# Row 0 of the first tile loaded from GpSimd's queue beside the other rows on SP's queue

## Chip, cores, metric

The kernel runs on one core of a Trainium2 chip. Times are device microseconds (us) of one launch; medians are given. The span of a profile is about 1.9 us shorter than the time of the same run. Kernels are compared only within the same rounds.

## The reference, cut to what matters

```python
# x: 1024 x 4096 float32, axis = -1
mean = np.mean(x, axis=axis, keepdims=True)
return ((x - mean) ** 2).astype(np.float32)
```

16.78 MB are read and 16.78 MB written, for very little arithmetic.

## The kernel before

There are two tiles of 128 partitions; each partition holds four rows (q = 0 to 3) of 4096 numbers, 64 KB. Both tiles are loaded at once, one DMA each ("load 1", "load 2"). VectorE sums a row, a tiny VectorE instruction turns the sum into the negative mean, ScalarE squares the row in place with the mean as bias. After rows 1 and 3 of each tile half a tile is stored: stores 1 and 2 of tile 1, 3 and 4 of tile 2. SP issues all of them into one queue. The loops, shortened:

```python
for i in range(ntiles):                      # ntiles = 2
    x_tile = io.tile([P, Q * D], F32)        # P = 128, Q = 4, D = 4096
    nc.sync.dma_start(out=x_tile, in_=x_t[i])
    tiles.append(x_tile)

for i in range(ntiles):
    for q in range(Q):
        row = tiles[i][:, q * D:(q + 1) * D]
        # ... neg_sum, neg_mean: [P, 1] tiles
        nc.vector.reduce_sum(out=neg_sum, in_=row, axis=..., negate=True)
        nc.vector.tensor_scalar_mul(out=neg_mean, in0=neg_sum, scalar1=inv_d)
        nc.scalar.activation(out=row, in_=row, func=Square, bias=neg_mean, scale=1.0)
        if q % H == H - 1:                   # H = 2
            part = slice((q + 1 - H) * D, (q + 1) * D)
            nc.sync.dma_start(out=out_t[i][:, part], in_=tiles[i][:, part])
```

Of the kernel before, what the change touches and what calls it, by code (L numbers as in the profile page):

```python
# [2 lines left out]

os.environ.setdefault("NEURON_RT_ULTRASERVER_MODE", "4")

# [4 lines left out]

F32 = mybir.dt.float32


@with_exitstack
def kernel(
    ctx: ExitStack,
    tc: tile.TileContext,
    x: bass.AP,
    axis: bass.AP,
    out: bass.AP,  # L20
):


    nc = tc.nc

    B, D = x.shape
    P = nc.NUM_PARTITIONS
    Q = 4
    H = 2
    assert B % (P * Q) == 0  # L30
    ntiles = B // (P * Q)
    inv_d = 1.0 / float(D)

    x_t = x.rearrange("(n p q) d -> n p (q d)", p=P, q=Q)
    out_t = out.rearrange("(n p q) d -> n p (q d)", p=P, q=Q)

    io = ctx.enter_context(tc.tile_pool(name="io", bufs=ntiles))
    stats = ctx.enter_context(tc.tile_pool(name="stats", bufs=2 * ntiles * Q))

    tiles = []  # L40
    for i in range(ntiles):
        x_tile = io.tile([P, Q * D], F32)
        nc.sync.dma_start(out=x_tile, in_=x_t[i])  # L43
        tiles.append(x_tile)

    for i in range(ntiles):
        for q in range(Q):
            row = tiles[i][:, q * D:(q + 1) * D]
            neg_sum = stats.tile([P, 1], F32)
            neg_mean = stats.tile([P, 1], F32)  # L50
            nc.vector.reduce_sum(  # L51
                out=neg_sum, in_=row, axis=mybir.AxisListType.X, negate=True
            )
            nc.vector.tensor_scalar_mul(out=neg_mean, in0=neg_sum, scalar1=inv_d)  # L54
            nc.scalar.activation(  # L55
                out=row,
                in_=row,
                func=mybir.ActivationFunctionType.Square,
                bias=neg_mean,
                scale=1.0,  # L60
            )
            if q % H == H - 1:
                part = slice((q + 1 - H) * D, (q + 1) * D)
                nc.sync.dma_start(out=out_t[i][:, part], in_=tiles[i][:, part])


# [1 line left out]
_INS = ['x', 'axis']  # L68
_OUTS = [((1024, 4096), 'float32')]

_NUMBERS = {'axis': -1}


# [26 lines left out]
```

## Time and profile before

| | before |
|---|---|
| time, median | 83.22 us |
| VectorE busy, of the span | 35.4 us, 44% |
| ScalarE busy | 30.7 us, 38% |
| DMA engines busy (mean of 16) | 96.2% |
| load 1 in, VectorE starts | 22.50 us |
| store 1 issued | 39.46 us |

Read it from the DMA side. The compute engines have gaps of many microseconds, the DMA engines none between 1.75 and 80.2 us. The prediction shows the lines. In the trace a "packet" is one contiguous piece that one of the 16 DMA engines moves, here one partition's part of a load or store. The records don't name the engine; a packet is put to the engine whose packet before ended as this one began. The engines pass from load 2 to store 1 at about 41.3 us.

### The profile page before, as it was taken

How to read it: one execution, taken by the hardware profiler on the slowest of the kernel's cores; microseconds unless marked ns; L12 is line 12 of the kernel's file. 1: busy time of each engine (PE TensorE's matmuls, PEld its weight loads, DVE VectorE, ACT ScalarE, POOL GpSimd, SP SyncE). 2: the span in 40 equal slices, each digit the busy share in tenths (PEclk: the TensorE clock that was granted, in tenths of full speed). 3: DMA queues.
4: the chain of work that ended last, by engine and by line, in shares of the span. 5: the costliest groups of instructions: out<-in, count | busy, mean ns of one | idle time of the engine just before them, and what ended most of it. 6: DMA issues, size and time to landing. Idle time of an engine off the chain costs nothing.

```text
span 81.3 us, 79 instructions
## 1 busy us (share of the span) xinstructions
DVE 35.4 (44%) x16; ACT 30.7 (38%) x9; POOL 0.2 (0%) x4
## 2 busy tenths in 40 slices
DVE  0000000000099999999749999999920000000000
ACT  0000000000060005969699930979879980000000
POOL 0000000000000000000000000000000000000000
DMA  9399947999965999992997997997998998898990
GB/s 387 129 516 516 516 193 322 516 516 516 516 290 226 516 516 516 516 483 129 419 516 306 467 516 322 451 516 338 435 516 354 419 516 387 387 516 387 403 500 0
DMA packets 864, 33.55 MB, mean 413 GB/s; under 512 B 96, under 2 KB 96, under 8 KB 96
## 3 DMA queue, kind: packets, MB, share of 16 engines
q1 hardware_dynamic: 864, 33.55, 96.2%
HBM read 16.78 MB, written 16.78 MB: 412 GB/s over the span
## 4 chain that ended last, share of the span: by engine, by line
DMA 50%; DVE 22%; ACT 5%; ACTq 4%; SPq 0%; issue 0%
DMA x_tile<-in_x_dram 50%; DVE neg_sum L51 21%; ACT x_tile L55 5%; ACTq L95 4%; SPq L43 0%; DVE neg_mean L54 0%
## 5 line engine op out<-in xcount | busy, mean ns | idle before, releaser
L51 DVE TENSOR_REDUCE neg_sum<-x_tile 128x1 f32<-128x4096 f32 x8 | 35.0, 4413 | 24.1 <-DMA x_tile<-in_x_dram 24.1
L55 ACT ACTIVATE x_tile<-x_tile,neg_mean 128x4096 f32<-128x4096 f32 x8 | 29.4, 3704 | 13.5 <-DVE neg_mean L54 13.5
L55 ACT ACT_TABLE_LOAD x1 | 1.3, 1283 | 22.5 <-DMA x_tile<-in_x_dram 22.5
L54 DVE TENSOR_SCALAR neg_mean<-neg_sum 128x1 f32<-128x1 f32 x8 | 1.1, 148 | 0.0
L81 POOL MEMSET const-bfloat16-1.0<- 128x1 bf16 x1 | 0.1, 101 | 0.0
L81 POOL MEMSET const-uint8-127<- 128x1 uint8 x1 | 0.1, 101 | 0.0
L81 POOL MEMSET const-float32-0.0<- 128x1 f32 x1 | 0.1, 98 | 0.2 <-issue 0.2
L81 POOL MEMSET const-float32-1.0<- 128x1 f32 x1 | 0.1, 98 | 0.0
## 6 DMA issues: line engine op xcount, KB each, us to landing
out_dram<-x_tile SPq DMA_DIRECT2D x4, 4096.0 KB, 12.9
x_tile<-in_x_dram SPq DMA_DIRECT2D x2, 31.2
```

The costliest lines, as they stand in the source:

```text
L51: nc.vector.reduce_sum(out=neg_sum, in_=row, axis=mybir.AxisListType.X, negate=True)
L54: nc.vector.tensor_scalar_mul(out=neg_mean, in0=neg_sum, scalar1=inv_d)
L55: nc.scalar.activation(out=row, in_=row, func=mybir.ActivationFunctionType.Square, bias=neg_mean, scale=1.0,)
L81: nc = _bacc.Bacc("TRN2", target_bir_lowering=False, num_devices=1)
L95: with _tile.TileContext(nc) as tc:
```

## The change

Its intent is that row 0 comes in early, so that VectorE can start before the whole tile is there.

```diff
-        nc.sync.dma_start(out=x_tile, in_=x_t[i])
+        if i == 0:
+            nc.gpsimd.dma_start(out=x_tile[:, :D], in_=x_t[i][:, :D])
+            nc.sync.dma_start(out=x_tile[:, D:], in_=x_t[i][:, D:])
+        else:
+            nc.sync.dma_start(out=x_tile, in_=x_t[i])
```

## The prediction

> **What bounds the kernel now.** I read the page from the top (busy shares, the slices, the DMA queue, the chain), then SP's waits, then the timeline, then the trace's records of single DMA packets. The first question for a load-compute-store kernel is whether its DMA engines ever run dry, because that decides whether an earlier start of the compute can be worth anything.
>
> ```profile
> DVE 35.4 (44%) x16; ACT 30.7 (38%) x9; POOL 0.2 (0%) x4
> ...
> DVE  0000000000099999999749999999920000000000
> ACT  0000000000060005969699930979879980000000
> POOL 0000000000000000000000000000000000000000
> DMA  9399947999965999992997997997998998898990
> ...
> DMA packets 864, 33.55 MB, mean 413 GB/s; under 512 B 96, under 2 KB 96, under 8 KB 96
> ...
> q1 hardware_dynamic: 864, 33.55, 96.2%
> ```
>
> No compute engine is busy for half of the span; the 16 DMA engines are busy for 96.2% of it, which is 0.962 x 81.3 = 78.2 us. Digits of 2, 3 or 4 in the DMA row look like holes. They are not: the packets are long against a slice of 2.03 us, and a slice in which few packets begin reads low while its neighbour reads too high. The packet records settle it. The loads are 256 packets of 64 KB (one per partition and tile), the stores 512 of 32 KB; the other 96 are the 4-byte semaphore writes, one per engine and transfer. A 64 KB packet takes 2.418 us (27.1 GB/s for an engine, 434 for 16), a 32 KB packet 1.213 us. The first packet of an engine begins between 1.75 and 2.27 us, and from there every engine's next packet begins at the end of the one before (a 64 KB packet every 2.414 us, no gap), through both loads and all four stores, until the last data packet ends at 80.2 us. The check: 33.55 MB in 80.2 - 1.75 = 78.45 us is 428 GB/s, 98.6% of 434. So one unbroken DMA stream sets the end.
>
> Next, what the compute engines wait for, and what SP, which issues everything, waits for. The chain of waits:
>
> ```profile
> by line: DMA x_tile<-in_x_dram 50.0%; DVE neg_sum L51 21.4%; ACT x_tile L55 4.6%; ACTq L95 4.4%; SPq L43 0.5%; DVE neg_mean L54 0.2%; issue 0.2%
> ```
>
> The same view piece by piece (start, length, what), which must be read with care:
>
> ```profile
> 1.16 40.64 DMA x_tile<-in_x_dram
> 41.80 0.02 issue
> 41.83 8.75 DVE neg_sum L51 x2
> ...
> 59.45 3.71 ACT x_tile L55
> 63.15 3.60 ACTq L95
> ```
>
> It ends at 66.8 us, at ACT's last Square, and leaves out the 13.4 us of stores after it. Taken literally it says that VectorE's sums cost 21% of the path. SP's waits (total, times, longest) show what is missing, the stores at the end, 13.3 us in the last line:
>
> ```profile
> SPq L64 <- ACT x_tile L55: 43.1, 4, 16.9
> SPq L64 <- DMA x_tile<-in_x_dram: 20.9, 1, 20.9
> SPq L95 <- DMA out_dram<-x_tile: 13.3, 2, 9.6
> ```
>
> Last, the timeline, for the first tile and the stores:
>
> ```profile
> 0.73 0.86 SPq L43 DMA_DIRECT2D x_tile<-in_x_dram  x2
> 22.50 8.75 DVE L51 TENSOR_REDUCE neg_sum<-x_tile 128x1 f32<-128x4096 f32 x2 [22.50 <-DMA x_tile<-in_x_dram]
> ...
> 39.46 27.65 SPq L64 DMA_DIRECT2D out_dram<-x_tile  x4
> ...
> 41.83 8.75 DVE L51 TENSOR_REDUCE neg_sum<-x_tile 128x1 f32<-128x4096 f32 x2 [1.62 <-DMA x_tile<-in_x_dram]
> ```
>
> The first store is issued at 39.46 us, while the engines still drain load 2 (to 41.4), so it is behind no hole. I check the other three by the ends of Square on ACT: store 2 at 40.11 + 7.31 = 47.4, store 3 at 55.06 + 3.71 = 58.8, store 4 at 66.8. The engines finish load 2 at 41.4, store 1 at 51.1, store 2 at 60.8, store 3 at 70.5 (8 packets x 1.213 = 9.7 us each). Each store is issued before its predecessor is through, with 1.9, 3.7, 2.0 and 3.7 us to spare. Compute is hidden, if narrowly.
>
> **What the Trainium skill says.** Four places, all on the page "DMA: Bandwidth & Descriptors". (1) Section "Issuing engines are not separate DMA queues": transfers started by the different engines run on the same 16 DMA engines and interleave; issuing from several saves sequencer time only. The trace has one queue, so it neither confirms nor denies this; what issuing could save is small, 0.86 us for both loads. (2) Section "Queues, rings and completion order": a DMA engine takes turns between the queues that have work, a whole packet at a time. Not shown here yet. (3) Section "Latency and other measured facts": about 0.6 us to the first byte for SP's path, about 1 us for GpSimd's. In the trace SP's issue begins at 0.73 and the first packet at 1.75, 1.0 us; GpSimd's has no example. (4) Section "Where 436 GB/s comes from": a ceiling of 435 GB/s for the 16 engines. The trace agrees: 434.
>
> **The change part by part.** Bytes: none added, none removed. Load 1 (8.39 MB as 128 packets of 64 KB) becomes 128 packets of 48 KB on SP's queue and 128 of 16 KB on GpSimd's; load 2 and the stores stay. At 27.1 GB/s a 48 KB packet is 1.81 us and a 16 KB one 0.605, together the 2.42 of before. Per engine that is 8 packets more, 24 instead of 16 for the loads. On one queue a further packet costs no gap that the trace shows; for the further packets and the turns between two queues I allow 0.01 (a semaphore write takes 0.009) to 0.05 us each, 8 times: 0.1 to 0.4 us. That is my choice, nothing in the trace measures it. 16 semaphore writes more at 9 ns cost nothing. SP still issues two loads, at about 0.4 us each; the third is issued on GpSimd, which has nothing else to do after its four memsets, done at 0.43 us.
> Start: SP's first packets leave at 1.75 as before, so the engines have work from then on whatever GpSimd does: 0. The first packet of an engine took 2.61 to 3.35 us, 3.06 in the mean, 0.64 over 2.418. A second queue could fill some of that start-up, so at best 0.5 us are won.
> Middle: row 0 lands early or not (below), VectorE may take its sum before 22.5, and then rows 1 to 3 end up to 4.4 us sooner. The instruction order also changes: the first mean follows the first sum at once, where before it came after the second. The most that comes of it is that store 1 is issued at about 35.0 (a sum of row 1 from 22.3, of row 2 to 31.1, a mean 0.14, Square 3.71) instead of 39.46. It stands behind load 2 on SP's queue, which drains to 41.4 either way. Worth: 0. Tile 2 starts at 41.8 when load 2 lands, unchanged, and so do stores 3 and 4.
> End: last packet at 80.2, then 1.1 us to the end of the span. A GpSimd queue in use may cost something in set-up or tear-down outside the stream; I allow 0 to 0.3.
> Sum: 83.22 + 0.25 (packets, queue turns) - 0.2 (start-up) + 0.1 = about 83.4.
>
> **The rivals.** First, when does row 0 land? Each engine has 8 small and 8 large packets. If it alternates whole packets, row 0 needs nearly all turns: 2.0 + 0.64 + 8 x 2.42 = 22.0 us, or 1.8 less if the small packet goes first in each turn; with some 0.4 to the wait's end, 20.5 to 22.4, and the intent of the change fails. If the two queues share by bytes, row 0 is through after twice its 8 x 0.605: 2.0 + 0.64 + 9.7 = 12.3. If a turn drains all of GpSimd's descriptors, about 2.0 + 3.06 + 4.8 = 10. I hold the first likeliest, as the profile counts a partition's row as one packet. All three leave the time where it is.
> Second, a gain from compute (4.4 us, to 78.8): the chain of waits speaks for it, VectorE's sums stand in it with 21%; the unbroken packets speak against it. It needs the DMA stream to have holes, and there is at most 1.0 us between the stream's 78.45 us and 33.55 MB at 434 GB/s, 77.4. So even the best stream gives 82.2, less than 2%.
> Third, GpSimd's queue is a burden: descriptors made late or in small pieces, a DMA engine that lags and holds back the last store. Only 2.1 of 33.55 MB are moved by it, 4.8 us of an engine's time; 20% worse would be 1.0 us, 84.2. Even arriving 10 us late costs nothing, since SP's queue fills the engines; it would only delay row 0, for which tile 1 has 1.9 us to spare.
>
> **Range and chances.** 83.4, with 82.8 (start-up filled, turns free) to 84.2 (third rival) for 8 in 10. Faster by over 2% needs below 81.6, which is less than the fastest stream allows: 0.01. Slower by over 2% needs 84.9, a small-packet cost of 1.7 us: 0.03. Within 2%: 0.96.
>
> **What would show it.** Right: DMA share of busy near 96%, some 94 to 97; two queues, GpSimd's with 2.1 MB; the last Square still near 66.8; VectorE waiting for load 2 until about 41.8; the first store issued between 35 and 40. Row 0's landing tells which rule of turns holds. Wrong: gaps between packets after row 0; stores that begin after their predecessor has drained; first packets much later than 1.75; an end longer than 1.1 us after the last packet.

## The result

The changed kernel takes 85.22 us (85.04 to 85.28), the kernel before in the same rounds 83.19. The ratio is 1.0237 (95% interval 1.0212 to 1.0261): slower. Ratios here are the mean time of one kernel's fast runs over that of the other's of the same rounds, so not quite the ratio of the medians quoted.

The page of the changed kernel, slices and queues:

```profile
DVE  0000000000008999999999999999900000000000
...
DMA  9299999977999659999059599979959996995990
...
DMA packets 1008, 33.55 MB, mean 402 GB/s; under 512 B 112, under 2 KB 112, under 8 KB 112
...
q1 hardware_dynamic: 864, 31.46, 88.2%
q0 software_dynamic: 144, 2.10, 5.9%
```

The bytes are the same. VectorE starts one slice later than before, not sooner. The two queues together are busy for 94.1% of a longer span, 78.6 us, against 78.2 before: the engines do the same work and have idled about 2 us more. A digit in the DMA row that is low only because few long packets begin in a slice looks the same as a real hole, so the row alone doesn't show where. The timeline of the changed kernel (start, length, engine, line, operation, and what ended the idle time):

```profile
1.22 0.65 POOL L44 DMA_DIRECT2D x_tile<-in_x_dram  x1 [0.78 <-PEq L99]
25.27 4.42 DVE L55 TENSOR_REDUCE neg_sum<-x_tile 128x1 f32<-128x4096 f32 x1 [25.27 <-DMA x_tile<-in_x_dram]
...
38.62 3.71 ACT L59 ACTIVATE x_tile<-x_tile,neg_mean 128x4096 f32<-128x4096 f32 x1 [5.00 <-DVE neg_mean L58]
42.36 25.93 SPq L68 DMA_DIRECT2D out_dram<-x_tile  x4
```

Row 0's sum starts at 25.27 instead of 22.50, 2.77 us later, and store 1 is issued at 42.36 instead of 39.46, 2.90 later. (The rest, 0.12, is the first mean, which now sits between the first two sums.) The issues with their times to landing say which load was late:

```profile
x_tile<-in_x_dram SPq DMA_DIRECT2D x1, 6144.0 KB, 21.5
x_tile<-in_x_dram POOLq DMA_DIRECT2D x1, 2048.0 KB, 24.0
x_tile<-in_x_dram SPq DMA_DIRECT2D x1, 41.0
```

The 2 MB of row 0 took longer to land than the 6 MB of rows 1 to 3. And this is the stretch around the passage from loads to stores, first in the kernel before, then in the changed one (window, length, busy time of VectorE, ScalarE and GpSimd with counts, clock, DMA share, GB/s):

```profile
41.30:43.20 1.90, 1.37 (x1) 1.90 (x1) 0.00 (x0) 1.00 0.96 414
43.20:80.20 37.00, 16.34 (x8) 18.94 (x6) 0.00 (x0) 1.00 0.98 425
```

```profile
41.30:43.20 1.90, 1.90 (x4) 1.22 (x2) 0.00 (x0) 1.00 0.00 0
43.20:82.30 39.10, 17.51 (x8) 21.84 (x6) 0.00 (x0) 1.00 1.00 429
```

For 1.9 us no data packet begins in the changed kernel. The packet records, as the mean of the 16 engines: loads done at 41.31 (before 41.26), first store packet at 43.26 (before 41.28), hence a hole (time of an engine between its last load packet and its first store packet) of 1.95 us against 0.01; the stores then take 38.95 us (before 38.74); the last one is done at 82.21 (before 80.01). So of 2.20 us in the profiled runs, 1.95 are the hole, 0.21 slightly slower stores, 0.05 the loads.

The chain of waits of the changed kernel gives VectorE's sums 41.6%, of the kernel before 21.4%:

```profile
by line: DVE neg_sum L55 41.6%; DMA x_tile<-in_x_dram 28.8%; ACT x_tile L59 4.4%; ACTq L99 4.3%; issue 0.8%; DVE neg_mean L58 0.7%; POOLq L99 0.0%; POOLq L85 0.0%
```

VectorE's busy time is 35.4 us in both. The chain follows VectorE further back because it no longer waits for load 2; it doesn't say that the sums cost more.

Why row 0 was late can be followed on one DMA engine. These are its packets in the changed kernel, put together from the trace's packet records (queue 1 is SP's, 0 GpSimd's; 4 B is the semaphore write that says "this engine's share has landed"):

```
1.761 to 4.115    queue 1  49152 B
4.111 to 5.929    queue 1  49152 B
5.925 to 6.536    queue 0  16384 B      first of row 0
6.532 to 8.347    queue 1  49152 B
...                                     strictly in turn
18.626 to 20.441  queue 1  49152 B      eighth and last of rows 1 to 3
20.438 to 21.049  queue 0  16384 B      seventh of row 0
21.045 to 21.054  queue 1  4 B          rows 1 to 3 done
21.051 to 21.662  queue 0  16384 B      eighth of row 0
21.658 to 24.076  queue 1  65536 B      load 2 begins
24.072 to 24.081  queue 0  4 B          row 0 done
```

The engine takes one packet of each queue in turn. GpSimd's queue got no packet in at the first turn (4.11) and stays one turn behind. Its last data was in at 21.66, but the semaphore write needs a turn of its own, and that came after a 64 KB packet of load 2: 2.42 us for four bytes. On all 16 engines the write comes after such a packet, on the last one at 24.85.

### The profile page after: what moved, and what is told of

It reads as the page before. It is cut to its first block, busy times and chain, and to the rows that moved or that the text cites. A ratio compares the mean times of both kernels' runs of the same rounds, so it can differ in the third digit from the quotient of the medians.

```text
span 83.5 us, 82 instructions
## 1 busy us (share of the span) xinstructions
DVE 35.4 (42%) x16; ACT 30.7 (37%) x9; POOL 0.8 (1%) x5
## 4 chain that ended last, share of the span: by engine, by line
DVE 42%; DMA 29%; ACT 4%; ACTq 4%; issue 1%; POOLq 0%
DVE neg_sum L55 42%; DMA x_tile<-in_x_dram 29%; ACT x_tile L59 4%; ACTq L99 4%; DVE neg_mean L58 1%; POOLq L99 0%; POOLq L85 0%
## 5 line engine op out<-in xcount | busy, mean ns | idle before, releaser
L44 POOL DMA_DIRECT2D x_tile<-in_x_dram x1 | 0.7, 652 | 0.8 <-PEq L99 0.8
```

The costliest lines, as they stand in the source:

```text
L44: nc.gpsimd.dma_start(out=x_tile[:, :D], in_=x_t[i][:, :D])
```

## The experiments

**Theory.** Row 0's completion is late through the turn of the semaphore write; VectorE works row 0 first and so starts late; store 1 comes after load 2 is through; the engines idle. **Main rival.** GpSimd's queue costs 2 us in itself, through set-up, slower packets or tear-down.

### e1: the same loads, row 0 worked last

```diff
-        for q in range(Q):
+        for k, q in enumerate((2, 3, 1, 0) if i == 0 else (0, 1, 2, 3)):
...
-            if q % H == H - 1:
-                part = slice((q + 1 - H) * D, (q + 1) * D)
+            if k % H == H - 1:
+                half = q // H
+                part = slice(half * H * D, (half + 1) * H * D)
```

> The changed kernel with the same loads on the same queues, but the rows of tile 1 worked in the order 2, 3, 1, 0, so that the row from GpSimd's queue is summed last; store 1 holds rows 2 and 3. Late-row theory (row 0 lands at 25.2 us, VectorE starts 2.8 us later, store 1 comes after load 2 has drained, the DMA engines idle 1.95 us each): VectorE starts at about 22.5, store 1 is issued near 39.5, the hole between load 2 and store 1 falls from 1.95 to under 0.1 us, time 83.3 (83.0 to 83.6). Rival, GpSimd's queue costs in itself (set-up, slowed packets, tear-down): 85.2, as the queue is used as before.

Measured: 83.52 us, before 83.27; ratio 1.0023 (1.0006 to 1.0041). The hole is 0.00. Row 0 is as late as in the changed kernel, 24.96 us, and costs nothing, as VectorE starts with row 2:

```profile
21.95 8.74 DVE L55 TENSOR_REDUCE neg_sum<-x_tile 128x1 f32<-128x4096 f32 x2 [21.95 <-DMA x_tile<-in_x_dram]
...
38.91 28.47 SPq L69 DMA_DIRECT2D out_dram<-x_tile  x4
```

So 1.8 of the 2.0 us are not GpSimd's queue as such: the rival falls. The remaining quarter of a microsecond is small, but the interval excludes a ratio of 1. In the packets, the last 64 KB packet of the engines took 2.57 us in the mean instead of 2.42, which explains 0.15 of it. More on that at e4.

### e2: load 2 cut into four loads of one row

```diff
         else:
-            nc.sync.dma_start(out=x_tile, in_=x_t[i])
+            for q in range(Q):
+                cols = slice(q * D, (q + 1) * D)
+                nc.sync.dma_start(out=x_tile[:, cols], in_=x_t[i][:, cols])
```

> The changed kernel with load 2 cut into four loads of one row each (16 KB packets instead of 64 KB); row 0 is still on GpSimd's queue and still worked first. Theory of the last turn (GpSimd's semaphore write stands one turn of SP's queue behind a 64 KB packet of load 2, 2.4 us): with 16 KB packets that turn takes 0.6, row 0 lands at about 23.4 instead of 25.24, VectorE starts near 23.5, store 1 is issued near 40.6, hole under 0.3 us, time 83.4 (83.1 to 83.8). Rival, only GpSimd's late first packet (5.9 us) is to blame, and the rival that the queue costs in itself: row 0 lands near 25 and the time stays at 85.2.

Measured: 83.60 us, before 83.27; ratio 1.0031 (1.0010 to 1.0052). Row 0, still from GpSimd's queue with its first packet at 5.9 us, and still worked first, has landed at 23.18, VectorE starts at 23.20, store 1 is issued at 40.29 and the hole is 0.01:

```profile
23.20 4.42 DVE L57 TENSOR_REDUCE neg_sum<-x_tile 128x1 f32<-128x4096 f32 x1 [23.20 <-DMA x_tile<-in_x_dram]
...
40.29 25.86 SPq L70 DMA_DIRECT2D out_dram<-x_tile  x4
```

The packet that the semaphore write stands behind is a quarter as long, and VectorE starts 2.07 us sooner; 1.81 of it are the shorter packet (2.42 - 0.61), most of the rest is row 0's last data, on the last engine in at 22.20 instead of 22.44. That shows the turn of the semaphore write, and that it is as long as the other queue's packet. Of the 0.33 us left against the kernel before, the packet records show 0.21 at the end of the loads and 0.08 in the stores.

### e3: row 0 from ScalarE's queue

```diff
-            nc.gpsimd.dma_start(out=x_tile[:, :D], in_=x_t[i][:, :D])
+            nc.scalar.dma_start(out=x_tile[:, :D], in_=x_t[i][:, :D])
```

> Row 0 from ScalarE's queue in place of GpSimd's, nothing else. If that queue has its first packets ready by the first turn, its eighth packet goes ahead of SP's semaphore write and its own semaphore write ahead of the first 64 KB packet: row 0 lands at about 22.3, VectorE starts near 22.5, store 1 near 39.6, time 83.3 (83.0 to 83.7). If it misses the first turn too, row 0 lands near 25 and the time is 85.2, as with GpSimd. That a second queue as such costs 2 us predicts 85.2 as well, but with row 0 early.

Measured: 83.81 us, before 83.27; ratio 1.0059 (1.0042 to 1.0076). The first packet of ScalarE's queue takes the first turn, at 4.20 us. The end of one engine's loads of tile 1 (queue 10 is ScalarE's):

```
19.320 to 21.135  queue 1   49152 B     eighth of rows 1 to 3
21.132 to 21.743  queue 10  16384 B     eighth of row 0
21.739 to 21.748  queue 1   4 B         rows 1 to 3 done
21.745 to 21.754  queue 10  4 B         row 0 done
21.751 to 24.169  queue 1   65536 B     load 2 begins
```

The last data of row 0 arrives no sooner than from GpSimd (21.74 against 21.66), but both semaphore writes go ahead of load 2. Row 0 has landed at 22.97, store 1 is issued at 40.08, the hole is 0.14. The time is 0.5 over before where I expected 0.1, just outside the range given: the loads end 0.17 us later, there is the hole, and the stores take 38.95 us, 0.21 more, as in the changed kernel. The 0.21 are not the second queue's: e6, with one queue, has the same 38.95, and e1, with GpSimd's queue, 38.72; the longer stores go with the larger holes. The hole itself was not due either, as store 1 is issued only 0.62 later than before and there was 1.0 to spare (worked out at e6): on four engines the first store packet came 1.5 to 1.8 us after the issue and 0.25 to 0.7 us after the loads; why is open. So what this second queue costs by itself is between 0.17 us and, if the hole is its doing, some 0.3, and it does not bring row 0 early either.

### e4: row 0 first on SP's own queue

```diff
-            nc.gpsimd.dma_start(out=x_tile[:, :D], in_=x_t[i][:, :D])
+            nc.sync.dma_start(out=x_tile[:, :D], in_=x_t[i][:, :D])
```

> Row 0 on SP's own queue ahead of rows 1 to 3: one queue, no turns. Row 0 lands near 7.5 us (1.9 + 0.6 + 8 x 0.605 + 0.4), VectorE starts there, rows 1 to 3 from about 22.4, store 1 is issued near 35.1, long before load 2 has drained. Theory that the unbroken DMA stream sets the end: no gain from the 15 us earlier start, 83.2 (82.9 to 83.5). Rival from the chain of waits (VectorE's sums set the end): 4.4 us gained, about 79.

Measured: 84.50 us, before 83.27; ratio 1.0143 (1.0117 to 1.0169). Both expectations miss. Row 0 is as early as one could wish, at 8.01 us, store 1 is issued at 35.13 without any hole, and the kernel is slower by 1.2 us:

```profile
8.04 4.42 DVE L55 TENSOR_REDUCE neg_sum<-x_tile 128x1 f32<-128x4096 f32 x1 [8.04 <-DMA x_tile<-in_x_dram]
...
35.13 33.52 SPq L68 DMA_DIRECT2D out_dram<-x_tile  x4
```

The windows (same columns as above):

```profile
38.50:42.20 3.70, 0.00 (x0) 3.70 (x2) 0.00 (x0) 1.00 1.02 283
42.20:81.80 39.60, 17.70 (x8) 15.61 (x5) 0.00 (x0) 1.00 0.98 424
```

From 38.5 to 42.2 us the engines are fully busy and move 283 GB/s. In the packet records it is exactly the last 64 KB packet of each engine, the one ahead of store 1: 3.43 to 4.09 us, 3.79 in the mean, instead of 2.42. The second theory, "the passage of the engines can also be spoilt by a store that is there too early", came from this run, and e5, e7, e8, e9 and e10 test it.

### e5: rows 1 to 3 in loads of one row, row 0 from GpSimd

```diff
-            nc.sync.dma_start(out=x_tile[:, D:], in_=x_t[i][:, D:])
+            for q in range(1, Q):
+                cols = slice(q * D, (q + 1) * D)
+                nc.sync.dma_start(out=x_tile[:, cols], in_=x_t[i][:, cols])
```

> The changed kernel with rows 1 to 3 in three loads of one row on SP's queue, so that both queues hold 16 KB packets and take equal turns. Row 0 then lands early, near 15 (a first GpSimd packet at about 5, then 8 pairs of 1.22), and store 1 near 33, far ahead of the end of load 2. If only a late store 1 costs time, no hole is left and the time is 83.4 (83.1 to 83.7). Rival, found in the run with row 0 first on SP's queue: a store that stands ready in the queue too early stretches the last 64 KB load packet of each engine (there 3.4 to 4.1 us instead of 2.42, 1.3 us in all): then the last packets are stretched here too and the time is 84.5. If that stretch belongs to one queue with row 0 ahead, it is absent here.

Measured: 84.38 us, before 83.21; ratio 1.0141 (1.0125 to 1.0156). With packets of equal size on both queues the turns do give row 0 early, at 15.24 us, as the change meant to. Store 1 is issued at 32.22, there is no hole, and the last load packets take 3.58 us in the mean. The first expectation (83.4) misses, the rival's came. So the stretch is not bound to one queue with row 0 ahead.

```profile
38.70:42.20 3.50, 0.00 (x0) 1.48 (x1) 0.00 (x0) 1.00 1.04 309
42.20:81.60 39.40, 17.71 (x8) 14.72 (x4) 0.00 (x0) 1.00 0.98 425
```

### e6: the kernel before with a late store 1

```diff
             neg_mean = stats.tile([P, 1], F32)
+            if i == 0 and q == 0:
+                extra = stats.tile([P, 1], F32)
+                nc.vector.reduce_sum(
+                    out=extra, in_=row[:, :D // 2], axis=mybir.AxisListType.X, negate=True
+                )
```

(One stats buffer more; the same in e7 and e9.)

> The kernel before, loads untouched, with one unused VectorE sum of half a row (about 2.3 us) ahead of row 0, which delays store 1 and nothing of the loads. Hole theory: store 1 is issued near 41.7, its first packet comes 0.85 later at 42.6, load 2 is through at 41.3 in the mean, so a hole of 1.2 to 1.4 us and 84.6 (84.2 to 84.9), with no second queue at all. Rival, the loss belongs to GpSimd's queue: 83.2.

Measured: 84.67 us, before 83.21; ratio 1.0179 (1.0162 to 1.0196). One queue, the loads of before, and 2.29 us of useless work on an engine that is busy for under half of the span cost 1.46 us:

```profile
22.59 2.29 DVE L53 TENSOR_REDUCE extra<-x_tile 128x1 f32<-128x2048 f32 x1 [22.59 <-DMA x_tile<-in_x_dram]
...
41.74 25.93 SPq L69 DMA_DIRECT2D out_dram<-x_tile  x4
```

Store 1 is issued at 41.74, its first packet begins at 42.59, the hole is 1.39. The 0.85 between issue and first packet is what makes the slack of the kernel before only 41.28 - 0.85 - 39.46 = 1.0 us. The changed kernel fits: 2.90 later, less 1.0, is 1.9.

### e7: e4 with a whole extra sum ahead of row 1

```diff
+            if i == 0 and q == 1:
+                extra = stats.tile([P, 1], F32)
+                nc.vector.reduce_sum(
+                    out=extra, in_=row, axis=mybir.AxisListType.X, negate=True
+                )
```

> Row 0 first on SP's queue as before, with one unused sum of a whole row (4.4 us) ahead of row 1, which moves store 1 from 35.1 to about 39.5. If a store waiting in the queue early stretches the last load packets, more work makes the kernel faster: last 64 KB packets near 2.43 us, 83.3 (83.0 to 83.6) against 84.5. Rival, that the split on one queue or its order costs the 1.3 us: 84.5 still, or more.

Measured: 83.13 us, before 83.21; ratio 0.9987 (0.9972 to 1.0002). The extra work makes e4 faster by 1.3 us, each against the kernel before of its own rounds. Store 1 is issued at 39.31, the last load packets take 2.43 us, the hole is 0.03:

```profile
38.50:41.00 2.50, 1.55 (x3) 1.82 (x2) 0.00 (x0) 1.00 0.97 419
41.00:80.20 39.20, 17.70 (x8) 20.99 (x6) 0.00 (x0) 1.00 0.99 428
```

Splitting the load on one queue costs nothing, then; the moment of store 1 does. (The extra sum also changes when VectorE and ScalarE work; e8 settles that rival.)

### e8: e4 with load 2 by rows

The edit is that of e4 and that of e2 together.

> Row 0 first on SP's queue, and load 2 in four loads of one row (16 KB packets); store 1 early, near 35. If the stretch is that of the one packet ahead of the store, it falls on a 16 KB packet (0.61 to about 1.0 us): loss under 0.5 us, 83.6. If it falls on a fixed time or number of bytes ahead of the store, 84.5.

Measured: 84.50 us, before 83.21; ratio 1.0148 (1.0131 to 1.0165): the second outcome. The last 16 KB packet of each engine takes 0.62 us, but the two before it 1.01 and 1.12 in the mean and the one before those 0.70, instead of 0.61: 1.0 us too much. The stretch belongs to about the last 64 KB ahead of the store, not to one packet; smaller packets don't help.

This run also answers a rival of e7, that the stretch goes with idle compute engines or with ScalarE's work and not with the store. In e4 and e5 VectorE is idle while the packets are stretched. Here tile 2 arrives by rows, and VectorE works on it all through the stretch:

```profile
35.10 25.86 SPq L70 DMA_DIRECT2D out_dram<-x_tile  x4
...
35.63 4.41 DVE L57 TENSOR_REDUCE neg_sum<-x_tile 128x1 f32<-128x4096 f32 x1
...
40.02 4.41 DVE L57 TENSOR_REDUCE neg_sum<-x_tile 128x1 f32<-128x4096 f32 x1
```

ScalarE is busy for 3.70 of 3.70 us in e4's window and for 1.48 of 3.50 in e5's, with nearly the same stretch. What the stretched runs share is the early store.

### e9: e4 with half an extra sum

The edit is that of e7 with `in_=row[:, :D // 2]`.

> Row 0 first on SP's queue with an unused sum of half a row (2.3 us) ahead of row 1: store 1 at about 37.4 instead of 35.1 or 39.5. Stretch of the last 64 KB load packets so far: 1.3 us in the mean of the engines with store 1 at 35.1, 0.14 at 38.9, 0.01 at 39.5. If it only asks whether the store's packets are in the queue when the last load packet begins (from 38.5 on; a store shows about 0.85 after its issue), the full 1.3 us stand at 37.4, 84.5. If it grows with the time that the store waits, about 0.6 us and 83.8.

Measured: 84.41 us, before 83.27; ratio 1.0131 (1.0105 to 1.0156). Store 1 is issued at 37.19, the last load packets take 3.85 us in the mean. The stretch is whole; it doesn't grow with the time that the store waits. It is there with store 1 issued at 37.19 or sooner, mostly gone at 38.91 (e1), gone at 39.31 (e7). As the last load packets begin between 38.5 and 39.1, it seems to ask whether the store was issued before they begin; but the change lies between 37.19 and 38.91, and no run has store 1 there.

### e10: e4 with stores 1 and 2 from ScalarE's queue

```diff
-                nc.sync.dma_start(out=out_t[i][:, part], in_=tiles[i][:, part])
+                (nc.scalar if i == 0 else nc.sync).dma_start(out=out_t[i][:, part], in_=tiles[i][:, part])
```

> Row 0 first on SP's queue, stores 1 and 2 issued from ScalarE's queue instead of SP's, so that store 1 need not stand behind load 2 but takes turns with it from about 36. If the stretch comes from a store waiting behind a load in one queue, load packets stay at 2.42 us; if from loads and stores mixing at the memory, every load packet after 36 is stretched. In either case load 2 lands some 2.4 us later (two store packets of 1.21 per engine go ahead), tile 2 is worked later, store 3 is issued near 61.2 while stores 1 and 2 are through at 60.8, so a new hole of about 1.2 us stands there: 84.4 without the stretch, more with it. A gain on 83.2 would show that the order of loads and stores has something left to give.

Measured: 85.79 us, before 83.27; ratio 1.0308 (1.0282 to 1.0333). Two losses, in the packet records: the load packet ahead of the first store packet takes 3.53 us in the mean, 1.11 too much, though it is in another queue; and between stores 2 and 3 there is the expected hole, 1.59 us, as load 2 landed later. The sum, 2.70, is near the 2.5 measured. The next load packet, which comes between two store packets, took 2.42 us again. So the stretch is neither "waiting behind in one queue" nor "loads and stores mixing" in general; it came at the first passage from a load to a store alone.

### All runs beside each other

Issue of store 1; last 64 KB load packet ahead of the first store, mean of 16 engines; hole between loads and stores.

| run | row 0 in | store 1 issued | last load packet | hole | time |
|---|---|---|---|---|---|
| e5 | 15.24 | 32.22 | 3.58 | 0.00 | 84.38 |
| e10 | 7.90 | 35.01 | 3.53 | 0 here, 1.59 later | 85.79 |
| e8 | 8.0 (VectorE starts at 8.03) | 35.10 | 16 KB packets, 1.0 too much | 0.00 | 84.50 |
| e4 | 8.01 | 35.13 | 3.79 | 0.00 | 84.50 |
| e9 | 7.89 | 37.19 | 3.85 | 0.00 | 84.41 |
| e1 | 24.96 | 38.91 | 2.57 | 0.00 | 83.52 |
| e7 | 7.85 | 39.31 | 2.43 | 0.03 | 83.13 |
| before | 22.48 | 39.46 | 2.43 | 0.01 | 83.2 |
| e3 | 22.97 | 40.08 | 2.42 | 0.14 | 83.81 |
| e2 | 23.18 | 40.29 | 16 KB packets, 0.61 | 0.01 | 83.60 |
| e6 | 22.57 | 41.74 | 2.42 | 1.39 | 84.67 |
| after | 25.24 | 42.36 | 2.42 | 1.95 | 85.22 |

The kernel before happens to sit at the best of the moments tried, as e7 does: store 1 is issued when the last load packets are under way, and more than 0.85 us before they end. No run beat it outside the noise; e7's interval includes 1.

What stays open: what the engine does in the stretched packets. The runs show when it comes and its size, 1.0 to 1.4 us, not its mechanism.

## Why the prediction was wrong

- "One unbroken DMA stream sets the end" was right, and so was the test named for the opposite, "stores that begin after their predecessor has drained". The error was that I took the stream for unbreakable. Of the signs of being right, the DMA share (94.1% against 94 to 97) and GpSimd's 2.1 MB came; store 1 between 35 and 40 us (42.36) and VectorE waiting for load 2 (no wait) did not.
- The step that failed is in the third rival: "Even arriving 10 us late costs nothing, since SP's queue fills the engines; it would only delay row 0, for which tile 1 has 1.9 us to spare." Both parts were wrong in size. Row 0 delayed store 1 by 2.90 us, and there were 1.0 us to spare, as a store's first packet comes 0.85 us after its issue (e6). The 1.9 was counted from issue to the end of load 2, though the prediction had itself measured 1.0 us from SP's first issue to its first packet. Late by 2.90 against 1.0 makes the hole of 1.95. For a time of 84.9 or more it gave a chance of 0.03, and only by costly small packets; that cost did not come.
- Ahead of it the term "with some 0.4 to the wait's end, 20.5 to 22.4" was too small: row 0 landed at 25.24. The last data of row 0 on the engine shown came at 21.66, close to the 22.0 worked out, and the rule of turns chosen as likeliest held. But the semaphore write takes a turn like any packet: another 2.42 us behind a 64 KB packet (e2 shrinks it, e3 avoids it, e1 makes it harmless).
- "The most that comes of it is that store 1 is issued at about 35.0 ... Worth: 0" was never reached, but e4 and e5 bring it about, and it is worth 1.2 us of loss. I had not thought of that.
- "For the further packets and the turns between two queues" 0.1 to 0.4 us were allowed: near the lower end or under it. The loads ended 0.05 us later with GpSimd's queue and 0.17 with ScalarE's; e7, with the split on one queue, shows no cost.
- "So at best 0.5 us are won" at the start: nothing was won. GpSimd's first packet came at 5.9 us, after the start-up was over (the first packets end at 4.1 to 4.9).
- The second rival, a gain from compute, is refuted as argued: e4 starts VectorE 14 us sooner, and no time is gained.
- Burden of GpSimd's queue itself: e1 is 0.25 us over before with all effects, inside the allowance, and 0.15 of that is the stretch.
- Two sums of the prediction are off in the last digit, without effect: 22.0 - 1.8 + 0.4 is 20.6, not 20.5, and 78.45 - 77.4 is 1.05, not "at most 1.0".

## What to carry to other kernels

Where DMA is the bound, ask of every change what it does to the moment at which the next transfer stands ready, counted from its issue to its first packet; the slack here was a microsecond, and once it was used up, 2.29 us of work on an engine that is busy for under half of the span cost 1.46 (e6). A small transfer on a second queue beside large packets wasn't early: it got one packet per turn, and its completion could need a turn of its own behind the other queue's next packet (after, e1, e2; not in e3). To have a piece early, put it first on the same queue, or give both queues packets of equal size, and then check what the earlier stores run into.

## What the Trainium skill lacked or had wrong

- "DMA: Bandwidth & Descriptors", "Queues, rings and completion order", says that an engine takes turns between queues packet by packet, with some 9 to 17 descriptors in a packet. The turns are as it says; in these records a turn was one partition's piece, 16 to 64 KB (of how many descriptors, they don't show). What the page lacks is that the semaphore write of 4 B took a turn of its own, which cost 2.42 us behind a 64 KB packet.
- The same page, "Latency and other measured facts", gives about 0.6 us to the first byte for SP's path and about 1 us for GpSimd's. SP's first packet began 1.0 us after its issue (0.74 to 1.76), a store's on idle engines 0.85 after (e6 41.74 to 42.59, the changed kernel 42.36 to 43.20). GpSimd's load was issued at 1.22 and had no packet ready when turns came at 4.1 to 4.9 us; in e5, with a turn about every 0.6 us, its first packets began at 5.43 to 5.73, over 4 us after the issue.
- No page has the stretch at the passage from loads to stores: a store issued 1.2 us or more before the load packets ahead of it begin lengthened about the last 64 KB of loads per engine by 1.0 to 1.4 us (e4, e5, e8, e9, e10), one issued 0.4 to 0.9 us after they had begun didn't (e7 and the kernel before).
